# Weights in whole units, gate projections in one place, nine units of room and a shared norm

## The chip, the cores and the metric

The kernel runs on one core of one Trainium2 chip. The number is the device time in microseconds of one execution. A core has TensorE (PE) for matrix products, VectorE (DVE), ScalarE (ACT) and GpSimd (POOL) for work on elements, and SyncE (SP), which here only issues DMAs. Sixteen DMA engines bring data from the chip's memory (DRAM) into the core's on-chip memory.

## The reference

Two blocks of a transformer follow each other, each of two layers, on 256 latent tokens and 256 context tokens of width 1024, in fp32. The first block has a multi-head latent attention mixer with a swiglu feed-forward layer, then a gated linear recurrence in both directions with a second swiglu layer. The second block has an even mixer (grouped attention and a pooling branch) and an odd mixer (neighbourhood attention), and behind each a layer of 32 experts. Cut to what matters here:

```python
# gated linear recurrence (layer 1 of the first block)
q, zf, zb, i, g = jnp.split(a @ w_in, 5, axis=-1)
... # two scans over the tokens give o, one head pair after the other in the kernel
out = (merge_heads(rms_norm(o, o_norm_w)) * silu(g)) @ w_o

# experts: 4 groups of 8, two experts a token, d_expert = 512
hb = jax.nn.silu(xb @ w1[e]) * (xb @ w3[e])
return hb @ w2[e]
```

The first layer of experts sees all 512 tokens, the second one only the 256 latent tokens. At the end stands an rms norm of the latent tokens.

## The kernel before

Activations lie with the features on the 128 partitions: 8 chunks of 128 features by 512 tokens (columns 0 to 255 context, 256 to 511 latent). In the dense layers fp32 accuracy comes from splitting both factors in a high and a low part (wh, wl of the weights, h, l of the activations) and three matmuls (L400 to L402); `split_w` makes wh on ACT (L329) and wl on DVE, in some places POOL (L330). The experts multiply plain fp32.

The stages follow each other: the dense stage "a" (attention, feed-forward, recurrence, feed-forward, even mixer), experts "0", the dense stage "b" (odd mixer), experts "1", the last norm. The products of the modulation vectors (the ada weights, L630) run as background work, a "tick" at a time, between the matmuls of the dense layers.

**Weights.** All large weights are cut into units of 1 MB, [128 x 2048] fp32, contiguous in DRAM. `raw` loads a unit as two half tiles of [128 x 1024], so 4 KB from each of 128 rows, with two DMAs on SP's queue (L310). The tiles rotate through pools: `ring` with RING = 6 units, `early` with EARLY = 5 units (second expert layer only) and `ring2` with 7 units (`experts(name, ck, ring2)`). An expert is six units: two halves of w1, of w3 and of w2. A load into a slot that has been used waits for the last matmul that read it. `fetch` issues loads ahead of their use: RING units ahead of experts "0", and EARLY + 1 + RING = 12 ahead of experts "1". SP issues its loads in program order, so one that waits holds back all behind it. The loads signal through eight completion semaphores in turn, and a load waits for the one that used its semaphore before it, so up to eight are in flight.

**Experts.** `moe` gathers each expert's tokens with a matmul (L1647), multiplies with w1 and w3 (`first`, L1668), applies silu and the product, transposes (L1685), multiplies with w2 (`second`, L1713), and puts the results back to the tokens with one more matmul each for the high and low part (L1733, L1734). Experts "0" takes two experts at a time, experts "1" four. `static` gives each unit its slot: `rings[(i - extra) % len(rings)]`. An overflow loop, which makes no round with these inputs, stands behind each layer and makes all engines wait for each other.

**Recurrence.** `hgrn` loops over four head pairs. For each it makes the two forget gates (take_z), q (take_q), the values V (`token_major`) and the output gate g (take_g), each from one unit of weights. Then it puts the rest of the work of that head pair, `hg_chain`, on a side list: eleven steps, nine of which are levels of a halving scheme (copies on ACT, L1031 to L1034; products on DVE, L1023; attention products on PE, L1051; a select on DVE, L1061). The linears of the next head pair call `step`, which advances the chain by one step after each of their outputs; `finish_side` runs what is left. The last chain is finished by `finish_side(1)`, with one tick of background work between two steps.

**Norm.** `full_rstd` squares eight chunks, on ACT (L483) or, for the chunks listed in `vector`, on DVE (L481), and sums them with matmuls of ones (L485).

**Order.** The program is written in Python and ordered by a scheduler that places the instructions of each engine by their dependencies and by the room in the pools; the order on each engine is then fixed.

Of the kernel before, what the change touches and what calls it, by code (L numbers as in the profile page):

```python
# [9 lines left out]
F32 = mybir.dt.float32  # L10
# [7 lines left out]
P = 128  # L18
# [225 lines left out]
class Net:  # L244
    def __init__(self, tc, I, out, cat, sat, ctx):
# [4 lines left out]
        self.sm = pool("sm", 16)  # L250
        self.ring = pool("ring", 2 * self.RING)
        self.psum = pool("psum", 8, space=PSUM)
        self.begin = ExitStack()
        self.dpool = self.begin.enter_context(tc.tile_pool(name="dpool", bufs=1))
        self.early = None
        self.ready, self.cut, self.background, self.side, self.due = {}, {}, [], [], []
# [12 lines left out]
    @contextmanager  # L269
    def experts(self, name, ck, ring2):  # L270
        tc = self.tc
        with tc.tile_pool(name=f"ck{name}", bufs=ck) as self.ck:
            with tc.tile_pool(name=f"ring{name}", bufs=2 * ring2) as self.ring2:
                with tc.tile_pool(name=f"r{name}", bufs=1) as self.rpool:
                    yield
# [24 lines left out]
    def raw(self, key, pool=None):  # L300

        if key in self.ready:
            return self.ready.pop(key)
        ap = self.I[key[0]][key[1:]] if len(key) > 1 else self.I[key[0]]
        n = ap.shape[-1]
        parts = []
        for i in range(0, n, 1024):
            w = min(n - i, 1024)
            t = (pool or self.ring).tile([P, 1024], F32, tag="raw", name="raw")
            self.nc.sync.dma_start(t[:, :w], ap[..., i : i + w])  # L310
            parts.append(t)
        return lambda lo, hi: parts[lo // 1024][:, lo % 1024 : lo % 1024 + hi - lo]

# [70 lines left out]
    def pair(self, pool=None):  # L384

        if pool:
            t = pool.tile([P, 1024], F32R, tag="raw", name="hl")
            return t[:, :512], t[:, 512:]
# [726 lines left out]
    def hgrn_(self, a, mod, hpool):  # L1115
# [9 lines left out]
        for hp in range(4):  # L1125
            base = hp * 5
            q = self.chunk(name="hq")
            g = self.chunk(name="hg")

            fc, kc, fl, kl = ([self.chunk(name=nm) for _ in range(2)] for nm in ("fc", "kc", "fl", "kl"))  # L1130

            def take_q(k, ps):
                nc.scalar.copy(q[:, k * S : (k + 1) * S], ps[:, :S])

            def take_g(k, ps):
                nc.scalar.activation(g[:, k * S : (k + 1) * S], ps[:, :S], AF.Sigmoid)
                nc.vector.tensor_tensor(g[:, k * S : (k + 1) * S], g[:, k * S : (k + 1) * S], ps[:, :S], op=ALU.mult)

# [18 lines left out]
            V = self.token_major(("hg_in", base + 3), 8, a, 1, 256)  # L1157
            self.linear([("hg_in", base + 4)], 8, 2, a, lat, take_g)
            G.append(g)
            self.finish_side()  # L1160
            self.side.append(self.hg_chain(hp, q, fc, kc, fl, kl, V, O, sums, mk, zero))
        self.finish_side(1)
        R = self.rows_rstd(sums, 3)
# [283 lines left out]
    def moe(self, l, entry, mod, segs, sl, after):  # L1447
# [290 lines left out]
        nxt = [0]  # L1738
        rings = [self.ring] * self.RING + [self.ring2] * (self.ring2.bufs // 2)
        extra = int(self.early is not None)  # L1740
        if self.early:
            rings = [self.early] * (self.early.bufs // 2) + rings

# [134 lines left out]
    def run(self):  # L1878
# [37 lines left out]
        with self.experts("0", 39, 7):  # L1916
            self.moe(0, entry, n0, whole, al, [("od_in", 4 + u) for u in range(4)] + [("od_in", u) for u in range(2)])
            r = self.full_rstd([self.X[:, k, al] for k in range(NC)], T)
        with self.tc.tile_pool(name="early", bufs=2 * self.EARLY) as self.early:
            with self.dense("b", 28):  # L1920
# [6 lines left out]
                entry.finish()  # L1927
            with self.experts("1", 12, 7):
                self.moe(1, entry, n1, latent, lat, [])
# [117 lines left out]
```

## Time and profile before

| what | value |
|---|---|
| median of 3 timed runs | 2674.04 us (2669.76 to 2677.62) |
| the profiled execution: its own time | 2669.05 us |
| its span | 2667.2 us |
| granted TensorE clock, mean (share of full speed) | 0.966 |
| PE busy | 2435.3 us (91%) |
| DVE busy | 1071.7 us (40%) |
| ACT busy | 802.5 us (30%) |
| POOL busy | 239.2 us (9%) |
| moved by DMA | 649.64 MB, mean 244 GB/s |

The span is the stretch of one execution that the profile covers. Busy shares are averages over all stages; the stages differ. Experts "0" lie between about 1455 and 1939 us, the dense stage "b" between about 1968 and 2190 us, and experts "1" between about 2190 and 2647 us of the span. A wait in the profile is idle time of an engine that ended when the named work ended.

### The profile page before, as it was taken

What the parts mean: (1) busy time and instruction counts of PE and PEld (TensorE: products, weight loads), DVE (VectorE), ACT (ScalarE), POOL (GpSimd) and SP (SyncE); (2) the same over time, 40 slices, a digit from 0 to 9 for tenths busy, and PEclk for the clock granted to TensorE, in tenths of its full rate; (3) what the DMA queues carried; (4) which work ended last, traced back from release to release, by engine and by line L of the source; (5) the groups of instructions that cost most, each with busy time, mean ns of one, the idle gap of its engine ahead of it and who ended that gap; (6) DMA issues with size and microseconds to landing.
All of it is one profiled execution on the core that took longest, in us unless ns stands there. A gap on an engine that the chain in (4) does not pass through costs nothing. (4 is left out here: it accounts for less than half of the span.)

```text
span 2667.2 us, 35570 instructions
## 1 busy us (share of the span) xinstructions
PE 2435.3 (91%) x13988; PEld 1628.6 (61%) x13988; DVE 1071.7 (40%) x2220; ACT 802.5 (30%) x1430; POOL 239.2 (9%) x217
## 2 busy tenths in 40 slices
PE   6999999999999989999998999999989988877775
PEld 3556678888699958996566544544459762222212
DVE  3456243232566665555664133333344741110102
ACT  4644242222444444445442111111134521000001
POOL 1000020101111122111112000000020000000000
PEclk9999999999999999999998999999989998988987
DMA  8158442222532276557613999999934459999996
GB/s 306 64 189 289 171 172 95 95 91 83 209 113 82 80 289 226 181 173 249 237 52 135 386 409 409 408 409 409 409 132 139 147 200 409 409 409 409 409 409 250
DMA packets 181057, 649.64 MB, mean 244 GB/s; under 512 B 19985, under 2 KB 21137, under 8 KB 180753
## 3 DMA queue, kind: packets, MB, share of 16 engines
q1 hardware_dynamic: 180608, 646.21, 64.6%
q8 instruction: 114, 1.87, 0.3%
q0 software_dynamic: 272, 1.05, 0.1%
q14 instruction: 63, 0.51, 0.1%
HBM read 646.13 MB, written 1.05 MB: 243 GB/s over the span
## 5 line engine op out<-in xcount | busy, mean ns | idle before, releaser
L400 PE MATMUL ps<-h,wh 128*128 128x512 f32 (+1 forms) x1396 | 482.1, 349 | 8.7 <-ACT h L565 7.2
L401 PE MATMUL ps<-l,wh 128*128 128x512 f32 (+1 forms) x1396 | 482.8, 346 | 4.0 <-DVE l L567 3.9
L1668 PE MATMUL w<-raw,xe 128*64 128x512 f32 (+1 forms) x2040 | 416.9, 656 | 74.7 <-DMA raw<-in_moe_w_dram 70.2
L402 PE MATMUL ps<-h,wl 128*128 128x512 f32 (+1 forms) x1396 | 481.6, 346 | 3.1 <-DVE wl L330 3.1
L330 DVE TENSOR_TENSOR wl<-raw,wh 128x1024 fp32r<-128x1024 f32 x254 | 310.7, 1244 | 165.8 <-ACT wh L329 161.9
L329 ACT CAST wh<-raw 128x1024 fp32r<-128x1024 f32 (+1 forms) x258 | 258.1, 1029 | 384.4 <-PE ps L401 300.5
L1668 PEld LDWEIGHTS w<-raw,xe 128*64 128x64 f32 (+1 forms) x2040 | 128.8, 131 | 341.0 <-issue 197.2
L400 PEld LDWEIGHTS ps<-h,wh 128*128 128x128 f32 x1396 | 265.3, 191 | 59.6 <-issue 13.9
L401 PEld LDWEIGHTS ps<-l,wh 128*128 128x128 f32 x1396 | 266.8, 191 | 39.1 <-DVE l L567 6.7
L402 PEld LDWEIGHTS ps<-h,wl 128*128 128x128 f32 x1396 | 266.6, 191 | 38.4 <-DVE wl L330 3.8
L1713 PE MATMUL y<-raw,ut 128*64 128x512 f32 (+1 forms) x1024 | 225.4, 597 | 31.1 <-ACT ut L1687 15.3
L1678 DVE TENSOR_TENSOR u<-u,w 128x512 f32<-128x512 f32 x24 | 16.5, 688 | 436.0 <-PE w L1668 436.0
L1713 PEld LDWEIGHTS y<-raw,ut 128*64 128x64 f32 (+1 forms) x1024 | 65.1, 123 | 171.9 <-issue 107.0
L1724 DVE SCALAR_TENSOR_TENSOR yl<-y,st,yh 128x512 fp32r<-128x512 f32 x48 | 35.5, 750 | 294.3 <-ACT yh L1723 202.5
L583 DVE SCALAR_TENSOR_TENSOR X<-ps,mod,X 128x256 f32<-128x256 f32 x120 | 53.5, 480 | 175.5 <-PE ps L402 175.5
L400 PE MATMUL ps<-uh,wh 128*128 128x512 f32 (+1 forms) x352 | 118.3, 336 | 0.0
L401 PE MATMUL ps<-ul,wh 128*128 128x512 f32 (+1 forms) x352 | 118.3, 336 | 0.0
L402 PE MATMUL ps<-uh,wl 128*128 128x512 f32 (+1 forms) x352 | 118.3, 336 | 0.0
L630 PE MATMUL ada<-raw,cs 128*32 128x512 f32 x768 | 112.3, 606 | 2.7 <-DMA raw<-in_ada_dram 2.6
L964 POOL TENSOR_TENSOR ul<-u,uh 128x512 fp32r<-128x512 f32 (+1 forms) x44 | 74.9, 1702 | 414.4 <-ACT uh L963 414.4
L960 DVE TENSOR_TENSOR u<-u,ps 128x512 f32<-128x512 f32 (+1 forms) x44 | 24.4, 555 | 206.1 <-PE ps L402 199.5
L1723 ACT ACTIVATE yh<-y,st 128x512 fp32r<-128x512 f32 x48 | 32.3, 686 | 237.4 <-PE y L1713 237.0
(372 smaller groups left out, 3498.8 us busy)
## 6 DMA issues: line engine op xcount, KB each, us to landing
raw<-in_moe_w_dram SPq DMA_DIRECT2D x766, 512.0 KB, 10.2
raw<-in_ada_dram SPq DMA_DIRECT2D x192, 512.0 KB, 5.4
raw<-in_ffn_dram SPq DMA_DIRECT2D x128, 512.0 KB, 4.6
raw<-in_hg_in_dram SPq DMA_DIRECT2D x40, 512.0 KB, 4.8
raw<-in_od_in_dram SPq DMA_DIRECT2D x24, 512.0 KB, 9.7
raw<-in_ev_in_dram SPq DMA_DIRECT2D x10, 512.0 KB, 6.3
raw<-in_mla_o_dram SPq DMA_DIRECT2D x8, 512.0 KB, 7.0
raw<-in_hg_o_dram SPq DMA_DIRECT2D x8, 512.0 KB, 9.9
```

The costliest lines, as they stand in the source:

```text
L329: self.nc.scalar.copy(h[:, c], rc)
L330: eng.tensor_tensor(l[:, c], rc, h[:, c].bitcast(F32), op=ALU.subtract)
L400: mm(out, w[0], a[0], start=start, stop=False)
L401: mm(out, w[0], a[1], start=False, stop=False)
L402: mm(out, w[1], a[0], start=False, stop=stop)
L583: self.nc.vector.scalar_tensor_tensor(x, ps[:, cs], self.m(mod, m, row)[:, k : k + 1], x, op0=ALU.mult, op1=ALU.add)
L630: nc.tensor.matmul(ps[32 * j : 32 * j + 32, :], self.cs[:, blk, k, :], r(j * 512, (j + 1) * 512), start=k == 0, stop=k == NC - 1,)
L964: nc.gpsimd.tensor_tensor(lo[:, :n], u, h[:, :n].bitcast(F32), op=ALU.subtract)
L1668: end = nc.tensor.matmul(ps[x * cap : (x + 1) * cap, :], xk[:, off + x * cap : off + (x + 1) * cap], wc[x], start=k == 0, stop=k == NC - 1,)
L1713: nc.tensor.matmul(ys[nh][x * cap : (x + 1) * cap, :], ut[:, hc * P + x * cap : hc * P + (x + 1) * cap], wc[x], start=hc == 0, stop=hc == 3,)
L1723: ACT.activation(yh[:], ys[nh][:], AF.Copy, scale=sw)
L1724: V.scalar_tensor_tensor(yl[:], ys[nh][:], sw, yh[:].bitcast(F32), op0=ALU.mult, op1=ALU.subtract)
```

## The change

- `raw` loads a unit into one tile of [128 x 2048] with one DMA of 1 MB, 8 KB from each row. The pools count whole units. The few small inputs that are loaded through `raw` (masks and the like) take a whole slot too.
- `pair`, which in one place takes tiles of the `early` pool for activations, now cuts a whole tile in two.
- The four gate projections of the recurrence (take_g) leave the loop over head pairs and become one linear over four units behind the loop, ahead of `finish_side(1)`.
- `ring2` of experts "1" has nine units where it had seven.
- The norm behind experts "0" has four of its eight squares on DVE.

```diff
--- before.py
+++ after.py
@@ -248,11 +248,11 @@
         pool = lambda name, bufs, **k: ctx.enter_context(tc.tile_pool(name=name, bufs=bufs, **k))
         self.cpool = pool("cpool", 1)
         self.sm = pool("sm", 16)
-        self.ring = pool("ring", 2 * self.RING)
+        self.ring = pool("ring", self.RING)
         self.psum = pool("psum", 8, space=PSUM)
         self.begin = ExitStack()
         self.dpool = self.begin.enter_context(tc.tile_pool(name="dpool", bufs=1))
-        self.early = None
+        self.early, self.halves = None, []
         self.ready, self.cut, self.background, self.side, self.due = {}, {}, [], [], []
         self.load_consts()
 
@@ -270,7 +270,7 @@
     def experts(self, name, ck, ring2):
         tc = self.tc
         with tc.tile_pool(name=f"ck{name}", bufs=ck) as self.ck:
-            with tc.tile_pool(name=f"ring{name}", bufs=2 * ring2) as self.ring2:
+            with tc.tile_pool(name=f"ring{name}", bufs=ring2) as self.ring2:
                 with tc.tile_pool(name=f"r{name}", bufs=1) as self.rpool:
                     yield
 
@@ -302,14 +302,9 @@
         if key in self.ready:
             return self.ready.pop(key)
         ap = self.I[key[0]][key[1:]] if len(key) > 1 else self.I[key[0]]
-        n = ap.shape[-1]
-        parts = []
-        for i in range(0, n, 1024):
-            w = min(n - i, 1024)
-            t = (pool or self.ring).tile([P, 1024], F32, tag="raw", name="raw")
-            self.nc.sync.dma_start(t[:, :w], ap[..., i : i + w])
-            parts.append(t)
-        return lambda lo, hi: parts[lo // 1024][:, lo % 1024 : lo % 1024 + hi - lo]
+        t = (pool or self.ring).tile([P, 2048], F32, tag="raw", name="raw")
+        self.nc.sync.dma_start(t[:, : ap.shape[-1]], ap)
+        return lambda lo, hi: t[:, lo:hi]
 
     def fetch(self, keys, pool=None):
         for k in keys:
@@ -384,7 +379,10 @@
     def pair(self, pool=None):
 
         if pool:
-            t = pool.tile([P, 1024], F32R, tag="raw", name="hl")
+            if not self.halves:
+                t = pool.tile([P, 2048], F32R, tag="raw", name="hl")
+                self.halves = [t[:, 1024:], t[:, :1024]]
+            t = self.halves.pop()
             return t[:, :512], t[:, 512:]
         return self.chunk(F32R, name="h"), self.chunk(F32R, name="l")
 
@@ -1125,16 +1123,11 @@
         for hp in range(4):
             base = hp * 5
             q = self.chunk(name="hq")
-            g = self.chunk(name="hg")
 
             fc, kc, fl, kl = ([self.chunk(name=nm) for _ in range(2)] for nm in ("fc", "kc", "fl", "kl"))
 
             def take_q(k, ps):
                 nc.scalar.copy(q[:, k * S : (k + 1) * S], ps[:, :S])
-
-            def take_g(k, ps):
-                nc.scalar.activation(g[:, k * S : (k + 1) * S], ps[:, :S], AF.Sigmoid)
-                nc.vector.tensor_tensor(g[:, k * S : (k + 1) * S], g[:, k * S : (k + 1) * S], ps[:, :S], op=ALU.mult)
 
             def take_z(d):
                 def take(k, ps):
@@ -1155,10 +1148,18 @@
             self.linear([("hg_in", base + 2)], 8, 2, a, slice(0, T), take_z(1))
             self.linear([("hg_in", base)], 8, 2, a, lat, take_q)
             V = self.token_major(("hg_in", base + 3), 8, a, 1, 256)
-            self.linear([("hg_in", base + 4)], 8, 2, a, lat, take_g)
-            G.append(g)
             self.finish_side()
             self.side.append(self.hg_chain(hp, q, fc, kc, fl, kl, V, O, sums, mk, zero))
+
+
+        def take_g(k, ps):
+            if k % 2 == 0:
+                G.append(self.chunk(name="hg"))
+            g, ks = G[-1], slice(k % 2 * S, (k % 2 + 1) * S)
+            nc.scalar.activation(g[:, ks], ps[:, :S], AF.Sigmoid)
+            nc.vector.tensor_tensor(g[:, ks], g[:, ks], ps[:, :S], op=ALU.mult)
+
+        self.linear([("hg_in", 5 * hp + 4) for hp in range(4)], 8, 2, a, lat, take_g)
         self.finish_side(1)
         R = self.rows_rstd(sums, 3)
         self.tick(4)
@@ -1736,10 +1737,10 @@
 
         kt, kr = keys(0.0), []
         nxt = [0]
-        rings = [self.ring] * self.RING + [self.ring2] * (self.ring2.bufs // 2)
+        rings = [self.ring] * self.RING + [self.ring2] * self.ring2.bufs
         extra = int(self.early is not None)
         if self.early:
-            rings = [self.early] * (self.early.bufs // 2) + rings
+            rings = [self.early] * self.early.bufs + rings
 
         def static(g):
             def get(nm, x, half):
@@ -1915,8 +1916,8 @@
         self.begin.close()
         with self.experts("0", 39, 7):
             self.moe(0, entry, n0, whole, al, [("od_in", 4 + u) for u in range(4)] + [("od_in", u) for u in range(2)])
-            r = self.full_rstd([self.X[:, k, al] for k in range(NC)], T)
-        with self.tc.tile_pool(name="early", bufs=2 * self.EARLY) as self.early:
+            r = self.full_rstd([self.X[:, k, al] for k in range(NC)], T, (1, 3, 5, 7))
+        with self.tc.tile_pool(name="early", bufs=self.EARLY) as self.early:
             with self.dense("b", 28):
                 self.pool_cuts = 2
                 a = self.modulated(n1, "nmix_1", 0, 1, whole, al, r, self.early)
@@ -1925,7 +1926,7 @@
                 )
                 self.fetch(self.expert_keys(1, 4)[self.EARLY + 1 : self.EARLY + 1 + self.RING])
                 entry.finish()
-            with self.experts("1", 12, 7):
+            with self.experts("1", 12, 9):
                 self.moe(1, entry, n1, latent, lat, [])
                 r = self.full_rstd([self.X[:, k, lat] for k in range(NC)], S, (1, 3, 5, 7))
                 ts = [self.chunk(name="fin") for k in range(NC // 2)]
```

In the new file the line numbers are lower by two to four from `raw` on.

Two places in the order of the instructions, one on SP and one on PE. On SP, the loads of the second expert layer from the point where its pool opens; DMAHW0 to DMAHW7 are the completion semaphores of earlier loads, and PE, DVE and Pool in the brackets are waits for these engines. Before:

```order
986 L310 DMA raw<-in_moe_w_dram 128x1024 [waits DMAHW5_49,DMAHW4_49,DMAHW7_49,PE_49,Pool_49]
987 L310 DMA raw<-in_moe_w_dram 128x1024
988 L310 DMA raw<-in_moe_w_dram 128x1024 [waits DMAHW6_49]
989 L310 DMA raw<-in_moe_w_dram 128x1024
990 L310 DMA raw<-in_moe_w_dram 128x1024 [waits DMAHW0_49]
991 L310 DMA raw<-in_moe_w_dram 128x1024 [waits DMAHW1_49]
...
998 L310 DMA raw<-in_moe_w_dram 128x1024 [waits DMAHW0_49]
999 L310 DMA raw<-in_moe_w_dram 128x1024 [waits DMAHW1_49]
1000 L310 DMA raw<-in_moe_w_dram 128x1024 [waits DMAHW2_49,PE_49]
```

After, the same place:

```order
561 L306 DMA raw<-in_moe_w_dram 128x2048 [waits DMAHW2_49,DMAHW1_49,DMAHW3_49,DMAHW0_49,DMAHW5_49,PE_49,Pool_49]
562 L306 DMA raw<-in_moe_w_dram 128x2048 x3
563 L306 DMA raw<-in_moe_w_dram 128x2048 [waits DMAHW4_49]
564 L306 DMA raw<-in_moe_w_dram 128x2048
565 L306 DMA raw<-in_moe_w_dram 128x2048 [waits DMAHW6_49]
566 L306 DMA raw<-in_moe_w_dram 128x2048 [waits DMAHW7_49]
567 L306 DMA raw<-in_moe_w_dram 128x2048 [waits DMAHW0_49]
568 L306 DMA raw<-in_moe_w_dram 128x2048 [waits DMAHW1_49,PE_49]
```

Between the first of these loads and the first that waits for PE again stood 14 half loads (986 to 999), seven units; now nine whole units stand there (561 to 567, with x3 in 562).

On PE, the end of the loop body of the recurrence for a head pair, where the chain of the head pair before it runs out: `ps` with `wh` and `wl` are the last matmuls of the projection that stands ahead of it, `att` the attention products of the levels (four to a level), `ho` the outputs of the chain. Before, the projection is the gate's (activations second):

```order
2987 L400 MATMUL ps<-h,wh 128x256
2988 L401 MATMUL ps<-l,wh 128x256
2989 L402 MATMUL ps<-h,wl 128x256
2990 L1051 MATMUL att<-qt,kt 128x128 x8
2991 L1099 MATMUL ho<-att,tm 128x128
2992 L1100 MATMUL ho<-Qf,states 128x128
```

After, it is that of the values V (weights second), and the gate's 48 matmuls stand behind the loop:

```order
2895 L398 MATMUL ps<-wh,h 128x256
2896 L399 MATMUL ps<-wl,h 128x256
2897 L400 MATMUL ps<-wh,l 128x256
2898 L1049 MATMUL att<-qt,kt 128x128 x12
2899 L1097 MATMUL ho<-att,tm 128x128
2900 L1098 MATMUL ho<-Qf,states 128x128
```

Two levels stood without other matmuls between them, and now three do.

## Rows read from the trace of the kernel before

**Rows 1.** Busy time by engine in the two expert stretches (window, length, then columns as named).

```profile
core 0: us, PE busy (x) PEld busy (x) DVE busy (x) ACT busy (x) POOL busy (x), PEclk, DMA share, GB/s
1455.00:1939.00 484.00, 469.54 (x2356) 239.24 (x2357) 148.28 (x338) 61.80 (x101) 1.22 (x1) 1.00 1.00 397
2190.00:2647.00 457.00, 351.47 (x1856) 116.06 (x1848) 49.92 (x130) 33.06 (x55) 1.09 (x2) 0.91 1.00 398
```

**Rows 2.** PE's waits, 2190 to 2647 us: us in total, times, longest us.

```profile
PE w L1668 <- DMA raw<-in_moe_w_dram: 66.7, 47, 2.2
PE y L1713 <- DMA raw<-in_moe_w_dram: 14.5, 22, 0.8
```

**Rows 3.** DMA view, 2200 to 2630 us.

```profile
DMA packets 48230, 175.81 MB, mean 409 GB/s; under 512 B 5361, under 2 KB 5361, under 8 KB 48209
...
raw<-in_moe_w_dram SPq DMA_DIRECT2D x335, 512.0 KB, 10.2
```

**Rows 4.** Windows at the start of the span, columns as in rows 1.

```profile
4.50:8.00 3.50, 0.00 (x0) 0.00 (x0) 0.78 (x4) 0.49 (x2) 0.00 (x0) 1.00 1.07 421
5.00:6.00 1.00, 0.00 (x0) 0.00 (x0) 0.78 (x4) 0.01 (x1) 0.00 (x0) 1.00 1.15 443
```

**Rows 5.** DMA view, 4.5 to 8 us.

```profile
DMA packets 154, 1.47 MB, mean 421 GB/s; under 512 B 17, under 2 KB 17, under 8 KB 75
```

**Rows 6.** DMA issues of the whole span: KB each, median us to landing.

```profile
X<-in_x_dram SPq DMA_DIRECT2D x1, 2048.0 KB, 9.7
```

**Rows 7.** SP's timeline around 2180 us: start, length, line, operation, count.

```profile
2170.09 12.08 SPq L310 DMA_DIRECT2D raw<-in_moe_w_dram  x14
...
2191.71 0.33 SPq L310 DMA_DIRECT2D raw<-in_moe_w_dram  x1
```

**Rows 8.** Windows behind the opening of experts "1", columns as in rows 1.

```profile
2192.00:2196.00 4.00, 4.00 (x34) 2.21 (x26) 0.00 (x0) 0.51 (x1) 0.00 (x0) 1.00 0.76 244
2196.00:2200.00 4.00, 4.00 (x37) 1.49 (x40) 0.00 (x0) 0.09 (x2) 0.00 (x0) 1.00 1.01 363
```

**Rows 9.** PE's timeline, last burst of expert products.

```profile
2640.18 3.62 PE L1713 MATMUL y<-raw,ut 128*32 128x512 f32 x20 [0.64 <-SPq L1804]
```

**Rows 10.** PE's waits, 1455 to 1939 us.

```profile
PE w L1668 <- DMA raw<-in_moe_w_dram: 3.5, 4, 1.5
```

**Rows 11.** Timelines of ACT, POOL and PE at the norm behind experts "0".

```profile
1950.22 4.27 ACT L483 ACTIVATE sq<-X 128x512 f32<-128x512 f32 x8 [6.88 <-POOL wl L330]
...
1940.58 9.37 POOL L330 TENSOR_TENSOR wl<-raw,wh 128x1024 fp32r<-128x1024 f32 x4 [484.36 <-ACT wh L329]
...
1950.91 4.68 PE L485 MATMUL s<-sq,cst 128*32 128x512 f32 x16 [5.25 <-ACT sq L483]
```

**Rows 12.** DVE's groups by shape, 780 to 944 us: busy us, mean ns, idle before.

```profile
L1019 DVE TENSOR_TENSOR Qf<-hq,fl 128x512 f32<-128x512 f32 x3 | 3.7, 1219 | 0.0
...
L1020 DVE TENSOR_TENSOR Qb<-hq,fl 128x512 f32<-128x512 f32 x3 | 2.0, 679 | 0.0
```

**Rows 13.** PE's timeline, the last norm's sums.

```profile
2652.08 1.93 PE L485 MATMUL s<-sq,cst 128*32 128x256 f32 x16 [5.33 <-issue]
```

**Rows 14.** PE's waits, 944 to 989 us.

```profile
PE spread L671 <- ACT rh L679: 2.9, 1, 2.9
PE ps L402 <- DVE wl L330: 2.9, 1, 2.9
PE adat L643 <- ACT adae L640: 2.0, 2, 1.3
```

**Rows 15.** PE's timeline at the end of a head pair.

```profile
811.43 1.95 PE L1051 MATMUL att<-qt,kt 128*128 128x128 f32 x16
```

**Rows 16.** DVE's groups of the chains, 780 to 944 us.

```profile
L1061 DVE COPY_PREDICATED att<-mk,att 128x512 f32<-128x512 uint8 x21 | 15.4, 732 | 6.7 <-PE att L1051 6.3
L1023 DVE TENSOR_TENSOR Qf<-Qf,Tf 128x256 f32<-128x256 f32 x20 | 8.3, 418 | 20.1 <-ACT qt L1031 20.1
```

**Rows 17.** PE's waits, 780 to 944 us.

```profile
PE osum L665 <- ACT sq L659: 1.2, 1, 1.2
```

## The prediction

> **What bounds the kernel now.** Start with the busy time of the engines in stretches of the span, because the page's single share for TensorE, 91%, is an average over stages with different limits. Two stretches move weights for experts [rows 1]. In the first one (1455 to 1939 us) PE is busy 469.54 of 484 us while the DMA share is 1.00: two limits lie on top of each other. In the last one (2190 to 2647 us) PE is busy only 351.47 of 457 us at a DMA share of 1.00. Next come PE's waits in that last stretch: the two longest entries, 66.7 and 14.5 us, are both waits for a raw weight tile [rows 2]. So 81 us of PE's idle time there end with a landing, and the stage takes as long as its weights take to come. The DMA view of 2200 to 2630 us says how fast that is: 409 GB/s, loads of 512 KB, nearly all packets below 8 KB [rows 3]. In the rest of the kernel the DMA has time to spare and PE is the bound, with short waits at the ends of dependent chains.
>
> **The stream of the last expert layer.** One expert is 6 units of 1 MB and there are 32, so 192 units. The code fetches 12 of them before the layer opens (EARLY + 1, then RING), and 180 are left. A unit is 1.0486 MB: at 409 GB/s that is 2.564 us. After the change each partition's piece of a load is 8 KB where it was 4 KB. The trace has one stretch with longer pieces: 4.5 to 8 us, where the loading of X (one load of 2 MB, 16 KB to a partition [rows 6]) runs beside a first weight load. There the DMA moves 421 GB/s [rows 4], and 154 packets carry 1.47 MB [rows 5]; only 75 of them are below 8 KB, so most of the bytes go in long ones. At 421 a unit takes 2.491 us, 0.073 us less, and 180 x 0.073 = 13.2 us. The bounds: nothing, if the rate stays 409; and 443 GB/s, the best single microsecond of that stretch [rows 4], which gives 2.367 us and 35 us in all. I take 421, the mean of the stretch, since a single microsecond holds too few packets.
>
> The Trainium skill, page "HBM Reference", section "Specifications (TRN2)", states that a core which streams alone measures about 425 GB/s and is bounded by its 16 DMA engines. No long stretch of this trace shows that; by it, as an estimate, a unit would take 2.467 us and the term would be 17.4 us.
>
> The Trainium skill also has a rule that speaks against a gain of this size: "DMA: Bandwidth & Descriptors", section "Why small descriptors are slow (HBM only)", puts the loss at about 3 fixed cycles to a packet beside one cycle for each 32 bytes. An estimate by it is 131 cycles for 4 KB and 259 for 8 KB, a saving of 1.15%, or 5.3 us on the 180 units.
>
> **Two more units of room.** SP issues 14 half loads from 2170.09 us for 12.08 us, to 2182.2, and its next one only at 2191.71 [rows 7]. By the order shown in the section on the change, that next one waits for PE, that is for the first used slot to come free. For 9.5 us nothing new is issued, and the queue runs dry: 244 GB/s in 2192 to 2196 and 363 in 2196 to 2200 [rows 8]. Against 409 that is (165 + 46) x 4 us = 0.84 MB, or 2.1 us of stream lost. With nine units of room two more units are issued ahead of the first wait for PE, 5.1 us of stream at 2.564 us each, more than the 2.1 us missing. So the hole closes: -2.1 us. The bound on the other side is 0, if PE's first use comes later by as much.
>
> **The coarser end.** A matmul now needs the whole unit where it needed half of it. Inside the stream that costs nothing, because PE waits for the stream anyway. At the end it shows. The last four units (four experts, last half of w2) are used in two passes over them, and the first pass could until now begin before the very last half had landed. The final burst is 20 matmul records in 3.62 us [rows 9], 0.18 us each; the eight matmuls of the first pass that now come behind the last landing cost 8 x 0.18 = +1.5 us, at most +2.9 if each has two records, at least 0. I take +1.5.
>
> **The first expert layer.** It has the same loads at the same rate, but PE is the other limit. PE's waits for raw tiles there add up to 3.5 us in 4 waits [rows 10]. A faster stream can take these away and no more; what is late next is PE itself. -3.5 us, bounds 0 and -3.5.
>
> **The norm behind the first expert layer.** ACT makes eight squares in 4.27 us, 0.53 each, and PE's 16 records of their sum take 4.68 us behind a wait of 5.25 [rows 11]. The change gives four squares to DVE. The nearest DVE rows, products of 128x512 in fp32, take 679 or 1219 ns [rows 12]: four of them 2.7 or 4.9 us. With 2.7 the squares would be ready 1.6 us earlier, with 4.9 they would be 0.6 us later. But PE has a floor: the same 16 records at 256 columns take 1.93 us [rows 13], so 3.9 at 512, and 4.68 can fall by 0.8. I take -0.8, bounds +0.6 and -1.6. The wait of 5.25 us ahead of it stays: it ends with ACT, which the split on POOL held up for 9.37 us [rows 11], and the change does not touch that.
>
> **The gates of the linear recurrence.** Nothing is added or removed: 4 x 48 matmuls, their 4 units of weights and the activation on each are moved from the loop over head pairs to one place after it. Two effects oppose each other. The chain of the last head pair now has those matmuls beside it. Between 944 and 989 us, where it runs out, PE waits 2.0 us for the ada transposes, 2.9 for the low part of a weight and 2.9 for the reciprocal roots [rows 14]; the last stands behind all chains and stays, so at most 4.9 us can go. Against that, inside the loop the gate's matmuls stood directly ahead of the last levels of the chain before. Now three levels stand back to back there where there were two. PE has about 0.98 us of work in a level (16 records in 1.95 us make two [rows 15]), while DVE needs four products of 0.42 us and one select of 0.73, 2.4 us [rows 16]. So a level without cover costs 2.4 - 1.0 = 1.4 us, 2.4 at most, for each of three chains: +4.2, at most +7.2. PE waits hardly anywhere in the loop today (1.2 us in 164 [rows 17]), so that cover is all used. The gain is at most -4.9 and the loss at most +7.2, and ACT and DVE may have run ahead far enough for neither. I take 0.
>
> **Sum.** -13.2 - 2.1 + 1.5 - 3.5 - 0.8 + 0 = -18.1 us. The profiled execution took 2669.05 us (span 2667.2 and 1.85 around it) and would come to 2651. It is the quickest of those shown; the median of the three timed runs is 2674.04, 5 us above. Put on the median the forecast is 2674.0 - 18.1 = 2656 us.
>
> **Rivals.**
> *The rate stays at 409.* The packets may be cut as before, or the engines may be at their limit whatever the length of a piece. For it: 409 is very even over hundreds of microseconds, as a hard limit would be. Against it: the 421 with longer pieces, over 3.5 us. Then both expert terms of the rate fall away and -2.1 + 1.5 - 0.8 = -1.4 is left: 2673 us.
> *Half of it.* The 421 is a mean over a short stretch that begins with empty queues, so only part of its 12 GB/s may be due to the length of a piece. At 415 GB/s a unit takes 2.527 us, the term is 6.7 us and the sum -11.6: 2662 us. The packet rule of the Trainium skill named above would give a result near this one.
> *More.* If the best microsecond is the true rate, the sum is -40: 2634 us. Against it: the rest of the same 3.5 us must lie below 421 to give that mean.
> *Slower.* The uncovered levels of the chains are the mechanism. Three chains with 2.4 us each give +7.2, the coarser end +2.9, the norm +0.6, the closed hole -2.1: +8.6, or 2683 us. It decides only if the rate does not rise, since 8.6 is less than 13.2. For it: the loop has no wait today and loses cover. Against it: the moved matmuls cover other waits later.
>
> **How the numbers follow.** The forecast has a chance of 0.62 (its own range 2646 to 2666), half of it 0.13, more 0.08, the rate that stays 0.12, slower 0.05. A measurement of this kernel can tell about 0.3%, 8 us, from no change. The forecast, the larger gain and most of the half are faster by more than that: 0.82. The rate that stays and the rest of the half are within it: 0.13. Slower: 0.05. The range for 8 in 10 leaves out the slower case and most of the larger gain and reaches to the unchanged rate: 2640 to 2672 us.
>
> **What the profile of the changed kernel would show.** Stream: in the last expert stretch the DMA view says 421 GB/s, not 409, and most packets are no longer below 8 KB; 409 there makes the first rival right. PE's waits for raw tiles there fall from 81 us to about 66. Room: no gap of 9 us between SP's loads after the layer opens and no slice below 400 GB/s. End: a final burst of PE behind the last landing that is longer than 3.62 us. First expert layer: PE's waits for raw tiles near 0, and its stretch some 3 us shorter; if it is shorter by much more, PE was not its limit. Norm: four squares on DVE, and PE's 16 records in about 3.9 us. Gates: PE waits behind the attention products inside the loop (against me if above 4 us) and shorter ones at its end. The prediction is wrong if the rate is not between 415 and 430, or if the dense stages together move by more than 6 us.

## The result, and the profile after

The changed kernel takes 2643.78 us (median of 4 runs, 2641.17 to 2645.61) against 2674.06 of the kernel before. The ratio is 0.9887, with a 95% interval of 0.987 to 0.9904: 30 us less, between 26 and 35. Forecast were 2656, with 2640 to 2672 as the range. The profiled execution took 2643.51 us (span 2641.6, clock 0.967).

Where the time went is read best by taking the same instruction in both traces and comparing its start. The table gives, for each stretch between two such instructions, by how many us it became longer (+) or shorter (-) than in the trace of the kernel before. "Units", "gates", "room" and "norm" are the kernel before with one part of the change alone; they and "ticks" are described below.

| stretch (us of the span before) | changed | changed, again | units | gates | room | norm | ticks |
|---|---|---|---|---|---|---|---|
| start, up to the first feed-forward layer (0 to 441) | +5.6 | +6.4 | +8.7 | +5.1 | +5.7 | +1.9 | +1.1 |
| recurrence and second feed-forward layer (704 to 1223) | -6.8 | -7.5 | -0.7 | -2.4 | 0.0 | +2.3 | +6.3 |
| even mixer and routing (1223 to 1455) | -1.0 | +0.1 | -0.5 | +3.7 | -1.0 | -2.0 | -3.5 |
| experts 0 (1455 to 1935) | -6.8 | -6.8 | -8.5 | -2.0 | -1.7 | -0.4 | -6.8 |
| norm behind them (1935 to 1960) | -1.0 | -1.0 | 0.0 | +0.3 | 0.0 | -0.5 | -0.8 |
| odd mixer (1960 to 2187) | +0.1 | +0.1 | -0.9 | +0.3 | -0.7 | +0.6 | +0.3 |
| experts 1 and last norm (2187 to 2658) | -15.4 | -15.2 | -10.3 | -0.6 | -4.7 | -0.2 | -15.0 |

Read it with care in two places. The first row scatters: "gates", "room" and "norm" have the start of the kernel before, and are 5.1, 5.7 and 1.9 us longer there, while "ticks", with the start of the changed kernel, is only 1.1 us longer (more on this under "The start"). The profiled execution of before was 5 us quicker than the median beside it, with the quickest start of all; that is why the two traces differ by 25.5 us and the medians by 30. And differences of 1 to 3.5 us in single stretches come up in kernels that change nothing there ("norm" in the recurrence, "gates" in experts 0, "ticks" in the even mixer). The entries for the experts stand out of that, and come back in the second trace of the changed kernel, as does that for the recurrence.

The stream first. The DMA view of 400 us of experts 1 in the changed kernel, the counterpart of [rows 3]:

```profile
DMA packets 23035, 167.82 MB, mean 420 GB/s; under 512 B 2564, under 2 KB 2564, under 8 KB 2564
...
raw<-in_moe_w_dram SPq DMA_DIRECT2D x159, 1024.0 KB, 19.9
```

420 GB/s where 409 stood, and packets below 8 KB are only the tiny ones. PE's waits there, the counterpart of [rows 2] (us in total, times, longest):

```profile
PE w L1669 <- DMA raw<-in_moe_w_dram: 61.3, 47, 1.5
PE y L1714 <- DMA raw<-in_moe_w_dram: 12.6, 22, 0.6
```

74 us instead of 81: the layer is still bound by its weights. I had expected about 66, the whole gain of the stage taken from these waits; part of it shows as PE's busy time instead (351.5 us in [rows 1], 343.6 in the same stretch now), and why was not looked into. In experts 0 PE waits for no weight any more (waits of 1440 to 1920 us, whole answer; [rows 10] before):

```profile
PE y L1714 <- ACT ut L1688: 10.5, 15, 0.7
PE pos L1555 <- DVE r L1551: 10.0, 1, 10.0
PE w L1669 <- ACT xe L1650: 3.4, 1, 3.4
```

The norm, counterpart of [rows 11 and 12]: PE's, ACT's and DVE's timelines (start, length, instruction, idle time before):

```profile
1941.91 3.65 PE L483 MATMUL s<-sq,cst 128*32 128x512 f32 x16 [5.21 <-ACT sq L481]
...
1941.22 2.19 ACT L481 ACTIVATE sq<-X 128x512 f32<-128x512 f32 x4 [6.89 <-POOL wl L325]
...
1941.31 2.49 DVE L479 TENSOR_TENSOR sq<-X 128x512 f32<-128x512 f32 x4
```

3.65 us instead of 4.68, behind the same wait (and less than the 3.9 that I had called PE's floor).

In the loop of the recurrence PE now waits behind the attention products (790 to 940 us; [rows 17] before), and where the last chain ends it waits less (965 to 1015 us; [rows 14] before):

```profile
PE att L1049 <- ACT kt L1032: 4.1, 4, 1.1
PE osum L663 <- ACT sq L657: 1.2, 1, 1.2
...
PE ps L398 <- ACT h L392: 3.3, 1, 3.3
PE spread L669 <- ACT rh L677: 2.1, 1, 2.1
PE adat L641 <- ACT adae L638: 1.2, 1, 1.2
```

### The profile page after: what moved, and what is told of

Same layout as the page of the kernel before. It is cut to its first block, busy times and chain, and to the rows that moved or that the text cites. A ratio compares the mean times of both kernels' runs of the same rounds, so it can differ in the third digit from the quotient of the medians.

```text
span 2641.6 us, 34288 instructions
## 1 busy us (share of the span) xinstructions
PE 2415.9 (91%) x13988; PEld 1625.0 (62%) x13988; DVE 1078.2 (41%) x2224; ACT 801.3 (30%) x1426; POOL 239.8 (9%) x217
## 5 line engine op out<-in xcount | busy, mean ns | idle before, releaser
L1669 PE MATMUL w<-raw,xe 128*64 128x512 f32 (+1 forms) x2040 | 410.1, 648 | 66.2 <-DMA raw<-in_moe_w_dram 61.3
```

Source lines behind the costliest of these rows:

```text
L1669: end = nc.tensor.matmul(ps[x * cap : (x + 1) * cap, :], xk[:, off + x * cap : off + (x + 1) * cap], wc[x], start=k == 0, stop=k == NC - 1,)
```

## The experiments

The theory was: each part has its own effect in its own stage, and they add. The rivals were that the parts need each other, that the rate is set by something else than the length of a partition's piece, and, for the recurrence, several causes. All ratios are to the kernel before, timed on the same chip.

**Units alone.** `raw`, the pools and `pair` as changed; the rest as before.

> The kernel before with whole units alone (one load of 1 MB with 8 KB to a partition; gates in the loop, seven units of room, squares on ACT). Theory A, that the gain is the sum of separate terms as the two traces show them by stage: start +5.6 us, experts 0 -6.8, experts 1 about -13 (420 GB/s instead of 409 over 180 units), in all about -14 us (-10 to -18). Theory B, that the parts need each other (the faster stream pays only with two more units of room): not more than -8 us. Both expect 420 GB/s in the DMA view of the expert layers.

Ratio 0.9937 (0.9924 to 0.995), -17 us; 420 GB/s in experts 1, 419 in experts 0. The faster stream pays without the other parts.

**Gates alone.** The take_g linear moved behind the loop; the rest as before.

> The kernel before with the gate projections behind the loop alone. Theory A: -7.5 us (the shift between the start of the recurrence and the end of the even mixer in the two traces), with about 4 us of new waits on PE at the attention products inside the loop and the waits of the last chain gone. Theory B, that this shift belongs to the whole units (fewer loads on SP, other landings) and the move itself is neutral, as forecast: 0 us, within 2.

Ratio 0.9993 (0.9984 to 1.0002), -2 us, which is within the interval of no change. Theory A failed: the 7 to 8 us of the changed kernel's recurrence are not there, though the 4.1 us of new waits in the loop are. In the trace the recurrence gains 2.4 us and the even mixer loses 3.7. What stands in the way in the recurrence is a wait at its end, from the waits of 965 to 1030 us:

```profile
PE spread L671 <- ACT rh L679: 6.9, 1, 6.9
PE ps L400 <- ACT h L394: 2.4, 1, 2.4
```

ACT's and DVE's timelines of this kernel show why:

```profile
974.88 0.63 ACT L467 ACTIVATE r<-v 128x512 f32<-128x512 f32 x1 [0.62 <-DVE v L466]
977.02 1.04 ACT L329 CAST wh<-raw 128x1024 fp32r<-128x1024 f32 x1 [1.51 <-DMA raw<-in_hg_o_dram]
978.08 1.28 ACT L468 ACT_TABLE_LOAD   x1
979.38 0.63 ACT L468 ACTIVATE r<-r 128x512 f32<-128x512 f32 x1
979.91 2.92 ACT L329 CAST wh<-raw 128x1024 fp32r<-128x1024 f32 x3
984.57 0.62 ACT L679 CAST rh<-r 128x512 fp32r<-128x512 f32 x1 [1.74 <-DVE r L471]
...
980.04 0.69 DVE L469 TENSOR_TENSOR q<-v,r 128x512 f32<-128x512 f32 x1 [0.71 <-ACT r L468]
980.97 1.22 DVE L330 TENSOR_TENSOR wl<-raw,wh 128x1024 fp32r<-128x1024 f32 x1 [0.24 <-ACT wh L329]
982.12 0.69 DVE L470 SCALAR_TENSOR_TENSOR q<-q,r 128x512 f32<-128x512 f32 x1
982.72 1.22 DVE L330 TENSOR_TENSOR wl<-raw,wh 128x1024 fp32r<-128x1024 f32 x1
983.85 0.69 DVE L471 SCALAR_TENSOR_TENSOR r<-q,r 128x512 f32<-128x512 f32 x1
```

and that of the changed kernel what is different:

```profile
974.85 0.63 ACT L465 ACTIVATE r<-v 128x512 f32<-128x512 f32 x1 [0.62 <-DVE v L464]
975.50 1.28 ACT L466 ACT_TABLE_LOAD   x1
976.79 0.63 ACT L466 ACTIVATE r<-r 128x512 f32<-128x512 f32 x1
977.61 1.99 ACT L324 CAST wh<-raw 128x1024 fp32r<-128x1024 f32 x2 [0.19 <-DMA raw<-in_hg_o_dram]
979.70 0.62 ACT L677 CAST rh<-r 128x512 fp32r<-128x512 f32 x1
...
977.45 0.69 DVE L467 TENSOR_TENSOR q<-v,r 128x512 f32<-128x512 f32 x1 [2.64 <-ACT r L466]
978.98 0.69 DVE L469 SCALAR_TENSOR_TENSOR r<-q,r 128x512 f32<-128x512 f32 x1
```

Both begin within 0.03 us of each other. With half loads a cast of the next weight stands between the two steps of the reciprocal root and waits there for a landing, so the second step ends 2.6 us later. Then two of DVE's splits of these weights (wl) stand between its three steps that finish the root: from the start of the first to the end of the last lie 4.5 us, and 2.2 in the changed kernel. `rh`, on which PE waits, comes 4.9 us later. The casts that stand ahead of `rh` on ACT do not hold it: ACT is idle for 1.74 us ahead of it and waits for DVE.

**Room alone.**

```diff
-            with self.experts("1", 12, 7):
+            with self.experts("1", 12, 9):
```

> The kernel before with nine units (18 half tiles) of room in experts 1 alone. Theory A: -2.1 us, the bytes missing in 2192 to 2200 us; no gap of SP's loads behind the opening of the layer and every slice of the stream at 409 GB/s. Theory B: 0, because PE's first use comes before the stream is needed; or -4 if the step between 2225 and 2260 us in the shift of the two traces belongs to the room.

Ratio 0.9991 (0.9982 to 1.0001), -2.4 us; in the trace -4.7 in experts 1, and as much (15.4 - 10.3 = 5.1) between the changed kernel and "units". The windows where the layer opens show the hole closed in this kernel, its answer to [rows 8]:

```profile
2174.00:2194.00 20.00, 12.46 (x89) 10.76 (x91) 14.58 (x79) 3.32 (x7) 2.81 (x3) 0.74 1.01 385
2194.00:2198.00 4.00, 4.00 (x33) 2.26 (x26) 0.00 (x0) 0.28 (x1) 0.00 (x0) 1.00 1.03 411
2198.00:2202.00 4.00, 4.00 (x38) 1.49 (x40) 0.00 (x0) 0.30 (x1) 0.00 (x0) 1.00 1.03 410
```

and the window ahead of those of [rows 8], in the kernel before, that the hole had begun earlier:

```profile
2172.00:2192.00 20.00, 12.46 (x91) 10.58 (x93) 14.36 (x79) 3.32 (x7) 2.59 (x3) 0.74 0.93 356
```

In the changed kernel it is not quite closed, and one slice stays far below 400 GB/s:

```profile
2182.00:2186.00 4.00, 4.00 (x34) 2.26 (x26) 0.00 (x0) 0.45 (x1) 0.00 (x0) 1.00 0.85 295
2186.00:2190.00 4.00, 4.00 (x38) 1.49 (x40) 0.00 (x0) 0.14 (x1) 0.00 (x0) 1.00 1.01 414
```

With whole units and seven of room ("units") the hole is deeper than before the change: 274, 8, 0 and 135 GB/s in the four stretches of 2 us from 2186 to 2194. Against 420 that is 2.5 MB or 6.0 us of stream, where the changed kernel lacks about 1.3 us. So two more units are worth more beside whole units.

**Norm alone.** `full_rstd(..., T, (1, 3, 5, 7))`; the rest as before.

> The kernel before with four of the eight squares on DVE alone. Theory A: -0.8 to -1.0 us, the step of the shift at that norm, too small for the times and to be read in the trace: PE's 16 records of the sum in about 3.9 us instead of 4.68. Rival: DVE's four squares end later than ACT's eight did, and the records take 4.7 us or more.

Ratio 0.9992 (0.9983 to 1.0002): not to be told from no change by the times. In the trace PE's 16 records take 4.15 us and the stretch is 0.5 us shorter.

**What sets the rate.** Three kernels, each the changed one with another way to fill a unit's tile. Two loads of 64 partitions:

```diff
-        self.nc.sync.dma_start(t[:, : ap.shape[-1]], ap)
+        for i in range(0, P, 64):
+            self.nc.sync.dma_start(t[i : i + 64, :n], ap[..., i : i + 64, :])
```

> The changed kernel with each unit as two loads of 64 partitions, 512 KB each, still 8 KB to a partition. If the length of a partition's piece sets the rate: 420 GB/s in both expert layers, as with one load. If the size or the number of the loads sets it: 409 GB/s, and some 13 to 20 us more than the changed kernel. The start may move by a few us in either case.

Neither: 3446.35 us, ratio 1.2902 (1.2849 to 1.2955). The stream of experts 0 begins at half the rate with all 16 engines busy (1500 to 1900 us, below), reaches 319 GB/s in 2200 to 2323 us, and in experts 1 it runs at 220 to 226. So this experiment does not separate the two:

```profile
DMA packets 13227, 86.87 MB, mean 217 GB/s; under 512 B 2634, under 2 KB 2634, under 8 KB 2634
...
q1 hardware_dynamic: 13212, 86.67, 99.7%
```

Two loads of 1024 columns, 4 KB to a partition, into the whole tile:

```diff
+        for i in range(0, n, 1024):
+            self.nc.sync.dma_start(t[:, i : min(i + 1024, n)], ap[..., i : min(i + 1024, n)])
```

> The changed kernel with each unit's tile filled by two loads of 1024 columns, 512 KB each, 4 KB to a partition; gates, room and norm as in the changed kernel. If the length of a piece sets the rate: 409 GB/s in both expert layers, the start as before the change, in all -7.5 (recurrence) - 2 (room) - 1 (norm) against the kernel before, about -10 us. If the whole tile (fewer slots to wait for) makes the rate: 420 GB/s and about 2637 us.

409 GB/s in both layers, ratio 0.9981 (0.9967 to 0.9996), -5 us. So the whole tile is not what makes the rate. The recurrence gave 3.4 us here and not 7.5, with the same cast ahead of the second step of the root as in "gates".

One load of 1 MB into two pieces of 4 KB a partition:

```diff
-        t = (pool or self.ring).tile([P, 2048], F32, tag="raw", name="raw")
-        self.nc.sync.dma_start(t[:, : ap.shape[-1]], ap)
+        t = (pool or self.ring).tile([P, 2, 1028], F32, tag="raw", name="raw")
+        self.nc.sync.dma_start(t[:, :, :1024], ap.rearrange("p (a b) -> p a b", a=2))
```

> The changed kernel with one load of 1 MB for a unit as there, but into a tile with 16 unused bytes between its halves, so that each partition gets two pieces of 4 KB instead of one of 8 KB. If the length of a piece sets the rate: about 409 GB/s and 44,000 packets in 400 us of an expert layer, as before the change. If the size or the number of the loads sets it: 420 GB/s.

One run, 2662.71 us. The DMA view of experts 0:

```profile
DMA packets 42540, 164.24 MB, mean 411 GB/s; under 512 B 2500, under 2 KB 2500, under 8 KB 42518
```

411 GB/s with loads of 1 MB, and 411 in experts 1 too. Of the 11 GB/s between 409 and 420, 9 come with the length of a piece and 2 with the size of the load.

**Ticks.** The changed kernel with `self.tick(8)` ahead of `finish_side(1)`, so that as much background work is done in the recurrence as before.

> The changed kernel with eight more ticks of background work directly behind the gate projections, ahead of the rest of the last chain: as many as the kernel before had done there. Theory A1, that the recurrence gained because these ticks, 1.06 us each, moved to the even mixer where they fill waits: about +7 us. Theory A2, that it gained because the gate products cover the last chain: 0 to +2 us, since the ticks are then missing from the even mixer's waits only.

Ratio 0.9927 (0.9913 to 0.9941), about 10 us slower than the changed kernel: on the side of A1, and beyond its 7 us. The experiment is not the ticks alone. Its recurrence is 13.1 us longer than in the changed kernel: PE is busy 8.8 us more, as eight ticks would have it, and idle 4.3 us more, with a wait of 4.8 us for a cast of a weight that the changed kernel does not have. In the changed kernel the last chain has advanced during the gate products, so fewer steps with a tick each are left, and seven ticks of 8 products (56 records, and four transposes) are done in the even mixer instead. PE's busy time from 704 to 1223 us falls by 7.7 us (500.96 to 493.3), and its idle time there is 18.0 us before and 18.9 after. In the even mixer the ticks cost little. The two windows of the even mixer and the routing, before and after:

```profile
1223.00:1455.40 232.40, 211.05 (x1202) 144.50 (x1198) 136.82 (x354) 97.44 (x196) 47.80 (x59) 0.95 0.46 167
```

```profile
1221.80:1453.20 231.40, 212.01 (x1262) 141.20 (x1258) 138.50 (x358) 97.77 (x197) 48.38 (x59) 0.98 0.54 203
```

60 more products on PE and 1 us less time here, but that is partly luck. Up to the same instruction, 0.4 us ahead of the end of these windows, the stretch takes 228.5 to 232.0 us in the five traces without these products (before, "units", "room", "norm", "ticks"), mean 230.6, and 230.9 to 236.5 in eight with them, mean 232.4, with "gates" the longest. So the seven ticks cost about 2 us there, and 7.7 us of busy time in the recurrence. PE's idle time in the stretch is 19.4 to 22.1 us without them and 16.4 to 19.8 with them. The granted clock of this stretch is 0.94 to 0.97 of full speed without them and 0.95 to 0.98 with them: it scatters by as much as between the two windows shown, and does not show that the products raise it.

**The cast order by itself.** The changed kernel with the four units of the recurrence's output projection as half loads.

```diff
+        w = 1024 if key[0] == "hg_o" else n
```

> The changed kernel with the four units of the recurrence's output projection alone loaded as two halves each. On ACT this puts the casts of these weights ahead of the end of the reciprocal roots, the order of the kernel before with the gates moved alone. Theory: this order is why the gates pay 6 us more with whole units than alone; PE's wait for the high part of the roots (rh) goes from 2.1 to 6.9 us and the stretch up to the second feed-forward layer is 4 to 6 us longer than in the changed kernel. Rival: the difference lies in the landings or in the start of the run; then the wait stays near 2 us.

PE's wait for `rh` is 6.7 us, 4.6 more than in the changed kernel, and the stretch from 704 to 1223 us is 7 us longer; where the other 2 us lie was not looked into:

```profile
PE spread L672 <- ACT rh L680: 6.7, 1, 6.7
```

Ratio 0.9916 (0.9902 to 0.9931), median 2649.92 beside 2646.04 of the changed kernel on that chip. The trace shows the effect; the times have it in the same direction, with intervals that overlap.

**The start.** The changed kernel with the first mixer's weights as half loads, then with all weights of the start.

```diff
+        w = 1024 if key[0].startswith("mla") else n
+        for i in range(0, n, w):
+            self.nc.sync.dma_start(t[:, i : min(i + w, n)], ap[..., i : min(i + w, n)])
```

> The changed kernel, with the loads of the first mixer alone (mla weights) as two halves of the whole tile. Theory A, that the start of the changed kernel lost 7.7 us because the first cast of a weight stands behind the split of the activations in ACT's order, 24th where it was 12th: it stands 12th again, the 8.15 us wait of PE ahead of the first dense product falls to about 2, and the whole is 5 to 7 us faster than the changed kernel, some 2637 us where that has 2644. Rival, that the loss is the landing of a whole unit itself (1.3 us later for the first one): 1 to 2 us faster.

> The changed kernel with all weights of the start (the first modulation vectors and the first mixer up to its values) as half loads into whole tiles. Theory: the first cast stands early on ACT again and the first ticks wait less for their weights; 3 to 6 us faster than the changed kernel, the quickest of all. Rival: what the start loses is caught up in the first mixer anyway; 0 to 2 us.

> The changed kernel once more, unchanged, as the base of the two beside it: 0.987 to 0.990 of the kernel before. Its trace tells how much of the shift of the first 440 us (5.6 us later than before in the first trace) comes and goes by itself: kernels with an unchanged start showed 0 to 6 us there.

Ratios: 0.9877 (0.9863 to 0.9891) for the first, 0.9881 (0.9863 to 0.9899) for the second, 0.9907 (0.9891 to 0.9924) for the changed kernel again on the second one's chip (medians 2640.06 and 2646.04). So the second is about 6 us quicker on the same chip (2637.81 to 2641.14 beside 2644.15 to 2650.84), though the intervals of the ratios touch. The first has no changed kernel on its chip beside it, and its ratio lies within the interval of the first result, 0.987 to 0.9904. What was lost at the start is seen in PE's waits of the changed kernel there:

```profile
PE ps L398 <- ACT wh L324: 8.2, 1, 8.2
PE ada L628 <- DMA raw<-in_ada_dram: 2.8, 2, 2.6
```

The cast that PE waits for begins on ACT at 44.92 us, with no idle time ahead of it:

```profile
44.43 0.58 ACT L555 ACTIVATE t<-t,mod,modA 128x256 f32<-128x256 f32 x1
44.92 1.03 ACT L324 CAST wh<-raw 128x1024 fp32r<-128x1024 f32 x1
```

Its unit had landed 8 us before. It stands behind most of the activations' split in ACT's order; with half loads it stands ahead of it, and in the second of these versions PE's wait there is 2.0 us, as before the change. With half loads in these two versions the first 441 us are 0.8 us longer than in the trace before; with whole units 5.6 and 6.4 in the changed kernel. These lengths alone decide nothing: two 512 KB loads to a unit throughout (the kernel with 4 KB pieces above) have +6.9, and "ticks" with whole units +1.1. PE's time there, divided in busy and idle, does. The windows of before, of the changed kernel and of "room" (columns as in [rows 1]):

```profile
0.00:441.00 441.00, 407.71 (x2057) 273.01 (x2058) 192.10 (x392) 189.49 (x342) 32.26 (x24) 0.99 0.53 189
0.00:446.60 446.60, 406.89 (x2056) 273.67 (x2057) 192.47 (x392) 189.69 (x342) 32.63 (x24) 0.97 0.49 185
0.00:446.70 446.70, 413.02 (x2057) 275.93 (x2058) 192.19 (x392) 189.58 (x342) 32.22 (x24) 0.97 0.52 186
```

PE is idle for 33.3 us in the first, 39.7 in the second and 33.7 in the third. Over all traces whose start comes in 128-partition loads it is idle for 33.3 to 34.9 us with half loads (seven traces) and for 38.1 to 39.9 with whole units (six). So whole units cost 3 to 7 us of waits at the start. The rest of the scatter is PE's busy time, 404 to 414 us for the same products, at a granted clock of 0.96 to 0.99.

## Why the prediction was right

The time lies in the range, and the mechanism of the likeliest case came true: the rate rose to 420. The time itself lies 2 us below that case's own range of 2646 to 2666, and the gain is 12 us larger than the sum. The dense stages together moved by -2 us in the trace, less than the 6 that I had named as a sign against me, but only because +5.6 at the start and -6.8 in the recurrence cancel. By its steps:

- *Stream, -13.2.* 420 GB/s for 421 forecast; at 420 the 180 units give -12.1. Right; that the length of the pieces sets it is shown above. That the figure fitted so well is partly luck: 421 was the mean of 4.5 to 8 us, with pieces of 16 KB, and the same trace has 412 in 4 to 8 us and 397 in 3 to 9. The rule of the Trainium skill ("DMA: Bandwidth & Descriptors", "Why small descriptors are slow (HBM only)"), by whose 3 cycles a packet an estimate of 1.15% was to be had, was too low: 409 to 420 is 2.7%. The figure of the Trainium skill's "HBM Reference", "Specifications (TRN2)", 425, is nearer.
- *Room, -2.1.* Mechanism right, size off: -4.7 and -5.1. I summed the missing bytes of 8 us. The stretch 2172 to 2192 had 356 GB/s where it can have 385, another 0.58 MB or 1.4 us, and 2200 to 2204 was still below 409. Beside whole units the hole to be closed was larger still, as shown above. Both signs that I named were wrong too: a slice of 295 GB/s stayed, and the gap between SP's loads did not go, it grew. In the changed kernel SP issues 9 loads from 2159.91 to 2165.0 and the next at 2183.5:

```profile
2159.91 5.13 SPq L306 DMA_DIRECT2D raw<-in_moe_w_dram  x9
...
2183.49 0.80 SPq L306 DMA_DIRECT2D raw<-in_moe_w_dram  x2
```

  But some 8 MB are under way as it begins, and last nearly to its end. What counts is the bytes in flight, not SP's gap.
- *Coarser end, +1.5.* Between the last landing and the start of the last expert product lie 1.8 us before and 3.1 after: +1.3. Right. The final burst is not longer, though, as I had named: it is the same 20 records in 3.62 us, and starts at the last landing instead of 1.2 us ahead of it.
- *Experts 0, bounded at -3.5.* It gave -6.8, beyond the bound. That step failed: PE's waits do not hold all the time that PE loses to its weights. The products of this layer are tiles of 128x64, and their records begin two at a time, a pair every 0.43 us: the 16 records of the second line below are eight pairs. Of the three in the first line, ahead of a wait, the last two begin alone, at 1778.81 and 1779.23 us, and each takes the 0.43 us of a pair. PE's timeline of the kernel before:

```profile
1778.43 1.39 PE L1668 MATMUL w<-raw,xe 128*64 128x512 f32 x3
1780.40 3.65 PE L1668 MATMUL w<-raw,xe 128*64 128x512 f32 x16 [0.57 <-DMA raw<-in_moe_w_dram]
```

  Two more begin alone at 1788.14 and 1788.57 us, and as many around the waits that end at 1846.92 and 1908.31; between 1500 and 1920 us of the changed kernel none does. Twelve records alone where six pairs would be: 2.6 us that count as busy. PE's busy time in the stretch fell by 3.3 us (469.54 to 466.23 with the same 2356 records), beside the 3.5 us of waits. And the shift between the two traces comes in three steps at these three places, 3.3, 1.7 and 1.8 us, and is level within 0.6 us between them. That it is the rate is shown by the kernels with 4 KB pieces and all else changed: +0.6 and -0.2 there.
- *Norm, -0.8.* -1.0 in both traces, -0.5 alone. Right; DVE's squares took 0.62 us each, near the shorter of the two rows.
- *Gates, 0.* Here the sum was right in the loop (+4.2 forecast, 4.1 of waits), though by another path: four waits of about 1 us for ACT's copies, in two of the three chains, where I had summed DVE's work for all three. The working failed at the end of the chain. I let it gain at most the 4.9 us of waits there. It gained by moving seven ticks to a stage that takes them nearly for nothing, which I had not counted, and it pays only if the casts of the next weight stay behind the reciprocal root. In all -7.8 and -7.4 in the two traces of the changed kernel; alone -2 by the times, not to be told from 0.
- *Start, not in the sum.* Whole units cost there: 3 to 7 us of PE's waits, and 6 us between the changed kernel and its second version with half loads. The prediction put this at nothing: it has no term for what the scheduler makes of later landings.

Three misses thus lie on one side (gates, experts 0 and the room) and one on the other (the start). The sum was nearer than its parts, by luck.

What stays open: why the scheduler puts the casts where it does. That splitting the loads alone moves them is shown at two places; that it goes by an expected landing is only argued. And why the granted clock, and with it PE's busy time at the start, differs between kernels with the same start was not looked into.

## What to carry to other kernels

For a stream that bounds a stage, make the contiguous piece for each partition long, and load small where something waits for the first piece: here large units for the experts with halves for the start took 2640 us, large units throughout 2646 on the same chip, and halves throughout 2670 on another. When a load changes its size, look at the order on the engines that consume it, since a scheduler may move the consumers. Price background work by the stage in which it ends up, and take the time that an engine loses to its data from the shift of whole stages, because around a wait records may run alone that elsewhere run in pairs, and that counts as busy.

## What the runs showed of the hardware beyond that

Loads that cover 64 of the 128 partitions moved 217 GB/s in 1500 to 1900 us, with the time of their packets at 99.7% of 16 engines' span (212 to 319 in stretches of experts 0), and loads over all 128 with the same piece of 8 KB 420. A 1 MB load in 4 KB pieces moved 411, two of 512 KB 409. PE's records for tiles of 128x64 began two at a time every 0.43 us, and alone at the same 0.43 us around waits.
